# Values of the first four heads later, the matmuls of two heads kept together for scores and for values, and the second norm's weights turned with the last forget sums

## The chip, the cores and the metric

The kernel runs on one core of one Trainium2 chip. The metric is the device time of one execution in microseconds (us), as the median of several runs of the same kernel. A core has five engines with instruction streams of their own, which wait for each other by semaphores: TensorE (PE in the profile; PEld is its weight load), VectorE (DVE), ScalarE (ACT), GpSimd (POOL) and SyncE (SP). DMA transfers are issued from the streams of SP, ACT and POOL.

## The reference

One inference step of a trunk with two layers, for 256 rows of a new stream (the prompt) and 8 running streams of 16 rows each (the sample), 384 rows in all and 2048 columns. Layer 0 projects the normed rows into eight forgetting-attention heads (fox) and eight stick-breaking heads, with queries, keys, values and gates, and writes keys and values out as well. Layer 1 is a gated MLP. The change touches layer 0, and in it mostly the fox heads:

```python
def fox_core(q, k, v, Fq, Fk, qpos, kpos):
    s = jnp.einsum('bqhd,bkhd->bhqk', q, k).astype(jnp.float32) * ATTN_SCALE
    s = s + (jnp.swapaxes(Fq, 1, 2)[..., :, None] - jnp.swapaxes(Fk, 1, 2)[..., None, :])
    causal = kpos[None, :] <= qpos[:, None]
    s = jnp.where(causal, s, -jnp.inf)
    p = jax.nn.softmax(s, axis=-1)
    return jnp.einsum('bhqk,bkhd->bqhd', p.astype(v.dtype), v)
...
for layer in range(DEPTH):
    if layer % 2 == 0:
        fq, fk, fv, fz, logf_p, sq, sk, sv, sz = ab_project(rmsnorm(hp, norm0_g), w_in0, b_forget)
        fo = fox_prompt(fq, fk, fv, logf_p)
        so = sb_prompt(sq, sk, sv)
        mix = jnp.concatenate([fo * jax.nn.silu(fz), so * jax.nn.silu(sz)], axis=-1)
        hp = hp + jnp.einsum('bsn,nd->bsd', mix, w_out0)
...
        k_all = jnp.concatenate([cache_fox_k.astype(gk.dtype), gk], axis=1)
        v_all = jnp.concatenate([cache_fox_v.astype(gv.dtype), gv], axis=1)
        F_all = jnp.cumsum(jnp.concatenate([cache_fox_logf.astype(jnp.float32), logf_s], axis=1), axis=1)
        go = fox_core(gq, k_all, v_all, F_all[:, P:], F_all, qpos, kpos)
...
    else:
        u, v, z = c_project(rmsnorm(hp, norm1_g), w_in1, sgu_ln_g, sgu_ln_b)
```

F is the running sum of the log forget gates. The sample rows attend to 128 cached rows of their stream and to their own; `norm1_g` is the weight vector of the second norm.

## The kernel before

**Projections.** Weights come from DRAM in pieces of 128 rows by 512 columns (`raw`, five buffers, SP's queue, L74). ACT rounds each to a high part (`whi`, L84) and DVE takes the rest as a low part (`wlo`, L86); the activations are split in the same way. `dense_nat` goes over the rows k of a weight two at a time, and `products` makes three products for each of the three blocks of 128 rows (prompt, prompt, sample): high by high (L100), high by low (L101), low by high (L102), 18 products for each pair of pieces, each 128x512. The text counts these large products to say where in PE's stream something stands.

**Quads.** `quad(g)` handles four heads: g = 0 and 1 are fox heads, 2 and 3 stick-breaking ones. It projects k, (v for g = 0), q, z, (v for g > 0). The work on the heads is put between the products of later projections: `at(g, what, kp, f)` registers f to be called in `dense_nat` of that quad and projection ahead of the pair of pieces kp (`between`). The table `places` says where each quad's four pieces go: scores of heads 0 and 1, scores of heads 2 and 3, then `attended` for the two pairs.

**A head** is a generator (`head`), driven by `scores` and `attended`. Its first part reads the running sums spread over the partitions (`fb`, L608 to L611, POOL's queue) and turns cached keys. Its second issues the prompt's score matmuls (L626, L627, L629), its third the cached ones (L632), the softmax (DVE L644, L645, L650, ACT L648) and the store of the attention weights to DRAM (`wd`, L667, ACT's queue). `scores` then reads them back in blocks for both heads of a pair (L492, four transfers on POOL's queue). The fourth part turns these blocks with DVE (L670, tile `PT`). The fifth makes the sample's value matmuls (L678 with own values, L682 with cached ones), the last the prompt's (L684 to L686) and the gating (L689). After it the result is stored (L504), and the cached values of a later head are read (L464). `mix_split` later splits a quad's gated results into high and low parts for the output projection.

**Forget sums.** For quad 0, `forget` is a generator that is called between products of the v projection. Its middle part sums the log forget gates by matmuls with a triangular matrix (L358 to L363 and two groups of four at L373), its last part transposes the sums (L383). Small matmuls write to PSUM banks from a pool of four (`bank`). `gains(j)` transposes the weights of norm j (PE, L164) into such a bank and copies them (DVE, L165) to `gT`.

**What sets the order.** The program is written in the Tile framework, whose scheduler orders the instructions of each engine by a model of their time and inserts the waits. `tc.issue_after(i)` is a context: what is written in it is put behind instruction i in the order of its own engine, which adds no wait of its own between engines.

Of the kernel before, what the change touches and what calls it, by code (L numbers as in the profile page):

```python
# [18 lines left out]
NT = 3  # L19
# [18 lines left out]
def tile_hybrid_step(  # L38
# [8 lines left out]
    V, S, G, PE = nc.vector, nc.scalar, nc.gpsimd, nc.tensor  # L47
# [45 lines left out]
    def products(out, his, los, ws, kp, tbs, first, last):  # L93

        for tb in tbs:
            t = slice(tb * P, (tb + 1) * P)
            for j, (hi, lo) in enumerate(ws):
                k = kp + j
                o = out[tb]
                PE.matmul(o, lhsT=his[k][:, t], rhs=hi[:, 0, :], start=(k == first), stop=False)  # L100
                PE.matmul(o, lhsT=his[k][:, t], rhs=lo[:, 0, :], start=False, stop=False)  # L101
                mm = PE.matmul(o, lhsT=los[k][:, t], rhs=hi[:, 0, :], start=False, stop=(k == last))  # L102
        return mm

    def dense_nat(w, k0, c0, his, los, nk=None, between=None, out=None, ks=None):


        nk = nk or len(his)
        out = out or [dbank() for _ in range(NT)]
        for kp in range(0, nk, 2) if ks is None else ks:  # L110
            behind = ()
            if between and kp in between:
                with tc.issue_after(splits[-1]), tc.issue_after(highs[-1]):
                    behind = between[kp]() or ()
            ws = [wunit(w[(k0 + k) * P:(k0 + k + 1) * P, c0:c0 + 512], 1, 512, behind=behind) for k in (kp, kp + 1)]
            products(out, his, los, ws, kp, range(NT), 0, nk - 1)
        return out

    def turn(src, dst, trn=None):
# [37 lines left out]
    with ExitStack() as l0:  # L157
# [4 lines left out]
        def gains(j):  # L162
            gb = bank()
            PE.transpose(gb[:, :KT], graw[:, j, :], ident[:KT, :KT])  # L164
            return V.tensor_copy(gT[:, j * KT:(j + 1) * KT], gb[:, :KT])  # L165
# [177 lines left out]
        def forget(o):  # L343
            z = lc.tile([P, NT, 8], F32, name="fz")
            for tb in range(NT):
                V.scalar_tensor_tensor(out=z[:, tb, :], in0=o[tb][:, 256:264], scalar=rstd[:, tb:tb + 1], in1=bfg, op0=ALU.mult, op1=ALU.add)
            e = lc.tile([P, NT, 8], F32, name="fe")
            S.activation(e, z, AF.Abs)
            S.activation(e, e, AF.Exp, scale=-1.0)
            S.activation(e, e, AF.Ln, bias=1.0)  # L350
            V.scalar_tensor_tensor(out=logf, in0=z, scalar=0.0, in1=e, op0=ALU.min, op1=ALU.subtract)
            G.dma_start(flf_p.rearrange("o (t p) h -> p (o t) h", p=P), logf[:, :2, :])
            G.dma_start(flf_s.rearrange("b q h -> (b q) h"), logf[:, 2, :])

            yield
            gains(1)
            b3 = bank()
            PE.matmul(b3[:8, :2 * P], lhsT=logf[:, 0, :], rhs=UT, start=True, stop=False)  # L358
            PE.matmul(b3[:8, P:2 * P], lhsT=logf[:, 1, :], rhs=UT[:, :P], start=False, stop=True)
            bs = bank()  # L360
            PE.matmul(bs[:8, :P], lhsT=logf[:, 2, :], rhs=BT, start=True, stop=True)
            for b_ in range(8):
                PE.matmul(bs[:8, P + b_:P + b_ + 1], lhsT=clf[:, b_, :], rhs=ones[:, 0:1], start=True, stop=True)  # L363
            tot = lc.tile([8, 8], F32, name="ftot")
            V.tensor_copy(tot, bs[:8, P:P + 8])
            FT = lp.tile([8, 2 * T], F32, tag="pr", name="FT")[:, :T]
            V.tensor_copy(FT[:, :2 * P], b3[:8, :2 * P])
            V.tensor_tensor(out=FT[:, 2 * P:].rearrange("h (b q) -> h b q", q=16), in0=bs[:8, :P].rearrange("h (b q) -> h b q", q=16),
                            in1=tot.unsqueeze(2).broadcast_to([8, 8, 16]), op=ALU.add)
            for hg in range(2):  # L370
                b5 = bank()
                for hh in range(4):
                    PE.matmul(b5[:8, hh * P:(hh + 1) * P], lhsT=clf[:, :, 4 * hg + hh], rhs=UT[:, :P], start=True, stop=True)  # L373
                hs = slice(4 * hg, 4 * hg + 4)
                b5v = b5[:8].rearrange("b (h p) -> b h p", p=P)
                nFc = lp.tile([8, 4, P], F32, tag="KT", bufs=4, name=nm("nFc"))
                S.activation(nFc, b5v, AF.Copy, scale=-1.0)
                G.dma_start(nFcd[:, hs, :], nFc)
            yield
            b4 = bank()  # L380
            for tb in range(NT):
                PE.transpose(b4[:, tb * 8:(tb + 1) * 8], FT[:, tb * P:(tb + 1) * P], ident[:8, :8])
            V.tensor_copy(Fnat, b4[:, :24].rearrange("p (t h) -> p t h", h=8))  # L383
            nFT = lp.tile([8, 2 * T], F32, tag="PT", name="nFT")[:, :T]
            V.tensor_scalar(out=nFT, in0=FT, scalar1=-1.0, scalar2=None, op0=ALU.mult)
            G.dma_start(nFd, nFT)
# [49 lines left out]
        def at(g, what, kp, f):  # L436
            plan.setdefault((g, what), {}).setdefault(kp, []).append(f)
# [28 lines left out]
        def quad(g):  # L466
# [11 lines left out]
            def scores(pair):  # L478

                for hh in pair:  # L480
                    hs = slice(hh * P, hh * P + P)
                    own[hh] = head(g, h0 + hh, own["k"][:, hh], lambda hs=hs: own["v"][:, :, hs], own["q"][:, hh],
                                   keys_of[4 * g + hh], lambda n=4 * g + hh: values_of[n], lambda hs=hs: own["z"][:, :, hs])
                wd = own[pair] = dram.tile([2, 6, P, P], F32, name=nm("wd"))
                for hh in pair[::-1]:
                    next(own[hh])
                for _ in range(2):
                    for j, hh in enumerate(pair):
                        own[hh].send(wd[j])
                blk = own["blk", pair] = slot(F32).rearrange("p (j x) -> p j x", j=2)  # L490
                for j in range(4):
                    G.dma_start(blk[32 * j:32 * j + 32].rearrange("p j (a d) -> p (j a) d", d=32),  # L492
                                wd[:, :, :, 32 * j:32 * j + 32].rearrange("j x (a p) d -> p (j x a) d", p=32))
                for hh in pair:
                    cached_keys(4 * g + hh + 2)

            def attended(pair):
                for j, hh in ((1, pair[1]), (0, pair[0])):
                    own[hh].send(own["blk", pair][:, j, :])
                for hh in pair:  # L500
                    next(own[hh])
                for hh in pair:
                    next(own[hh], None)
                    G.dma_start(own["d"][hh].rearrange("(t p) c -> p t c", p=P), own["z"][:, :, hh * P:hh * P + P])  # L504
                for hh in pair:
                    cached_values(4 * g + hh + 2)
                if pair[0]:
                    mixed.append(blocks(own["d"])[0])


            places = ((("z", 12), ("k", 2), ("k", 8), ("k", 12)), (("z", 12), ("v", 2), ("k", 2), ("k", 8)))[g > 0]
            at(g, "q", 2 if g == 0 else 14, lambda: turned("k"))
            at(g, "z", 12, lambda: turned("q"))
            for i, (what, kp) in enumerate(places):
                at(g + (what == "k"), what, kp, lambda i=i: (scores, attended)[i // 2](((0, 1), (2, 3))[i % 2]))
            at(g + 1, "q", (12, 8, 8, 8)[g], lambda: mix_split())

            def evict(o, dst, scale, n=512):
                for tb in range(NT):
# [67 lines left out]
        def mix_split():  # L587
            blk = mixed.pop(0)
            mT = big("vnat").rearrange("p t c -> p (t c)").rearrange("p (k t) -> p k t", k=4)
            V.transpose(out=mT.rearrange("p k t -> p (k t)"), in_=blk.rearrange("p k t -> p (k t)"))  # L590
            hi, lo = slot().rearrange("p (k t) -> p k t", k=4), slot().rearrange("p (k t) -> p k t", k=4)
            for k in range(4):
                S.activation(hi[:, k, :], mT[:, k, :], AF.Copy)
                V.tensor_tensor(out=lo[:, k, :], in0=mT[:, k, :], in1=f32(hi[:, k, :]), op=ALU.subtract)
                mh.append(hi[:, k, :])
                ml.append(lo[:, k, :])
# [4 lines left out]
        def head(g, h, kT, values, qT, kc, vc, gate):  # L601
# [65 lines left out]
            nc.scalar.dma_start(wd.rearrange("x q k -> q x k"), weights.rearrange("q (x k) -> q x k", k=P))  # L667
            blk = yield
            PT = lp.tile([P, 2 * T], F32, tag="PT", name=nm("PT"))
            V.transpose(out=PT, in_=blk)  # L670
            yield
            PD = PT[:, T:]
            vn, vc, z = values(), vc(), gate()
            ob = bank()
# [317 lines left out]
```

## Time and profile before

| | us |
|---|---|
| runs | 1812.33, 1813.67, 1812.5 |
| median of the three | 1812.5 |
| profiled execution, its own time | 1815.39 |
| its span, from the first to the last instruction | 1813.7 |
| mean granted TensorE clock over the span | 0.995 |

The profiled execution is one more run of the same kernel, with the profiler on; its time contains 1.7 us beside the span. In its rows "a<-b" is an output tile and its inputs, "x8" the number of instructions taken together, and a bracket at the end of a timeline row holds the idle time of the engine just before, and whose end it waited for. The profile's line numbers are those of the kernel before; in the changed kernel the same lines stand 2 or 3 further down, except in the forget sums, where the shift is 1 (L373 is L374) after `gains(1)` is gone.

### The profile page before, as it was taken

How to read it: one execution, taken by the hardware profiler on the slowest of the kernel's cores; microseconds unless marked ns; L12 is line 12 of the kernel's file. 1: busy time of each engine (PE TensorE's matmuls, PEld its weight loads, DVE VectorE, ACT ScalarE, POOL GpSimd, SP SyncE). 2: the span in 40 equal slices, each digit the busy share in tenths (PEclk: the TensorE clock that was granted, in tenths of full speed). 3: DMA queues.
4: the chain of work that ended last, by engine and by line, in shares of the span. 5: the costliest groups of instructions: out<-in, count | busy, mean ns of one | idle time of the engine just before them, and what ended most of it. 6: DMA issues, size and time to landing. Idle time of an engine off the chain costs nothing. (4 is left out here: it accounts for less than half of the span.)

```text
span 1813.7 us, 24384 instructions
## 1 busy us (share of the span) xinstructions
PE 1788.8 (99%) x8575; PEld 1483.8 (82%) x8575; DVE 924.2 (51%) x1538; ACT 710.2 (39%) x1261; POOL 369.9 (20%) x544
## 2 busy tenths in 40 slices
PE   9999799999999999999999999999999999999998
PEld 8988588888888888888888888888888888888887
DVE  6337356458448455543433544554544563455366
ACT  5435236337337344433333333333333333333334
POOL 1515524313312202200300120320130210220020
PEclk9999899999999999999999999999999999999999
DMA  6868778878876877644444444454544554555553
GB/s 195 233 179 212 201 216 216 251 196 206 238 207 179 241 204 207 189 128 128 135 129 131 138 137 146 148 146 130 157 143 128 146 154 128 145 146 150 164 145 117
DMA packets 185771, 307.63 MB, mean 170 GB/s; under 512 B 22904, under 2 KB 63152, under 8 KB 185648
## 3 DMA queue, kind: packets, MB, share of 16 engines
q1 hardware_dynamic: 127696, 225.37, 42.1%
q0 software_dynamic: 25072, 63.53, 14.1%
q10 hardware_dynamic: 32880, 17.18, 3.2%
q8 instruction: 67, 1.10, 0.3%
q14 instruction: 56, 0.46, 0.1%
HBM read 269.23 MB, written 30.47 MB: 165 GB/s over the span
## 5 line engine op out<-in xcount | busy, mean ns | idle before, releaser
L86 DVE TENSOR_TENSOR wlo<-raw,whi 128x512 fp32r<-128x512 f32 x784 | 538.0, 695 | 745.1 <-ACT whi L84 744.9
L101 PE MATMUL d<-wlo,slot 128*128 128x512 f32 x2349 | 916.6, 391 | 0.2
L102 PE MATMUL d<-whi,slot 128*128 128x512 f32 x2349 | 912.0, 389 | 0.0
L84 ACT ACTIVATE whi<-raw 128x512 fp32r<-128x512 f32 x784 | 493.4, 631 | 944.9 <-PE d L102 889.3
L100 PE MATMUL d<-whi,slot 128*128 128x512 f32 x2349 | 822.9, 391 | 0.0
L100 PEld LDWEIGHTS d<-whi,slot 128*128 128x128 f32 x2349 | 440.9, 188 | 94.3 <-ACT whi L84 1.6
L101 PEld LDWEIGHTS d<-wlo,slot 128*128 128x128 f32 x2349 | 441.0, 188 | 91.7 <-DVE wlo L86 1.0
L102 PEld LDWEIGHTS d<-whi,slot 128*128 128x128 f32 x2349 | 441.0, 188 | 91.5
L126 POOL DMA_DIRECT2D gTt<-trn x128 | 78.0, 618 | 446.0 <-issue 263.9
L396 POOL DMA_DIRECT2D slot<-d x48 | 44.1, 924 | 145.9 <-DVE wlo L86 53.6
L492 POOL DMA_DIRECT2D slot<-wd x32 | 29.4, 924 | 103.4 <-DMA wd<-pr 34.6
L833 POOL DMA_DIRECT2D wr<-in_w_sp_dram x64 | 34.9, 553 | 26.2 <-DVE wT L837 25.1
L826 DVE TENSOR_TENSOR slot<-d,slot 128x512 f32<-128x512 f32 x48 | 32.0, 686 | 12.4 <-PE d L102 12.4
L783 POOL DMA_DIRECT2D slot<-in_sgu_ln_g_dram x8 | 4.5, 567 | 135.5 <-PE d L102 135.5
L455 POOL DMA_DIRECT2D kcache<-in_cache_sb_k_dram x32 | 24.9, 786 | 32.4 <-DVE KT L621 32.4
L455 POOL DMA_DIRECT2D kcache<-in_cache_fox_k_dram x32 | 25.0, 789 | 23.4 <-DVE KT L621 22.2
L709 POOL DMA_DIRECT2D blk<-h1d x12 | 11.0, 919 | 70.7 <-DMA h1d<-slot 60.4
L799 POOL DMA_DIRECT2D bcol<-in_b_sp_dram x1 | 1.2, 1176 | 116.1 <-DVE w L798 116.1
L862 PE MATMUL a<-vt,wT 128*128 128x256 f32 x96 | 24.5, 380 | 0.0
L777 POOL TENSOR_SCALAR rsv<-mvr 128x3 f32<-128x3 f32 x1 | 0.5, 540 | 113.0 <-DVE mvr L776 113.0
L774 DVE BATCH_NORM_STATS2 stats<-vt 128x6 f32<-128x512 f32 x24 | 16.3, 690 | 11.4 <-ACT vt L773 11.4
L849 DVE SCALAR_TENSOR_TENSOR gate<-d,rstd,gate 128x512 f32<-128x512 f32 x24 | 17.4, 748 | 7.3 <-PE d L102 7.3
(239 smaller groups left out, 1201.3 us busy)
## 6 DMA issues: line engine op xcount, KB each, us to landing
raw<-in_w_in_dram SPq DMA_DIRECT2D x640, 256.0 KB, 2.8
raw<-in_w_out_dram SPq DMA_DIRECT2D x189, 256.0 KB, 3.4
slot<-d POOLq DMA_DIRECT2D x48, 192.0 KB, 6.2
d<-slot ACTq DMA_DIRECT2D x24, 256.0 KB, 3.9
wd<-pr ACTq DMA_DIRECT2D x16, 384.0 KB, 5.8
slot<-wd POOLq DMA_DIRECT2D x32, 192.0 KB, 5.3
gTt<-trn POOLq DMA_DIRECT2D x128, 48.0 KB, 3.5
kcache<-in_cache_fox_k_dram POOLq DMA_DIRECT2D x32, 128.0 KB, 5.8
```

Source lines behind the costliest of these rows:

```text
L84: highs.append(S.activation(hi, raw, AF.Copy).ins)
L86: splits.append(V.tensor_tensor(out=lo, in0=raw, in1=f32(hi), op=ALU.subtract).ins)
L100: PE.matmul(o, lhsT=his[k][:, t], rhs=hi[:, 0, :], start=(k == first), stop=False)
L101: PE.matmul(o, lhsT=his[k][:, t], rhs=lo[:, 0, :], start=False, stop=False)
L102: mm = PE.matmul(o, lhsT=los[k][:, t], rhs=hi[:, 0, :], start=False, stop=(k == last))
L126: G.dma_start(dst[32 * j:32 * j + 32, :, 32 * a:32 * a + 32], trn[32 * a:32 * a + 32, :, 32 * j:32 * j + 32])
L396: r = G.dma_start(blk[32 * j:32 * j + 32].rearrange("p h (a d) -> p (h a) d", d=32), d[:, :, 32 * j:32 * j + 32].rearrange("h (a p) d -> p ...
L455: G.dma_start(k[32 * j:32 * j + 32].rearrange("p (b d) -> p b d", d=32), (c_fox_k, c_sb_k)[n // 8][:, :, n % 8, 32 * j:32 * j + 32].rearra ...
L492: G.dma_start(blk[32 * j:32 * j + 32].rearrange("p j (a d) -> p (j a) d", d=32), wd[:, :, :, 32 * j:32 * j + 32].rearrange("j x (a p) d -> ...
L826: evicted = V.tensor_tensor(out=h1[c][:, tb, :], in0=o[tb], in1=h1[c][:, tb, :], op=ALU.add)
L833: G.dma_start(wr[js, 0, :].rearrange("p (a s) -> p a s", s=32), w_sp[g, :, js].rearrange("(a p) s -> p a s", p=32))
L862: PE.matmul(m[:, i * 256:(i + 1) * 256], lhsT=wTs[i][:, tb // 2, :], rhs=vt[:, tb, cs], start=True, stop=True)
```

## The change

Four things are changed. `gains(1)` moves from the head of the forget sums to behind the last forget transposes. In `scores`, the prompt's score matmuls of both heads of a pair are put behind the last large product that had been written. In `attended`, the matmuls of the first head are put behind the turning of both heads' weights. And the places of quad 0 change: `attended` of heads 0 and 1 from k, 8 of the next quad to k, 12, that of heads 2 and 3 from k, 12 to q, 4, and the first quad's `mix_split` from q, 12 to z, 4. The places of the other quads stay (they are written in another form).

```diff
+    last_product = []
...
-            products(out, his, los, ws, kp, range(NT), 0, nk - 1)
+            last_product[:] = [products(out, his, los, ws, kp, range(NT), 0, nk - 1).ins]
...
             yield
-            gains(1)
             b3 = bank()
...
             V.tensor_copy(Fnat, b4[:, :24].rearrange("p (t h) -> p t h", h=8))
+            gains(1)
...
                 for hh in pair[::-1]:
                     next(own[hh])
-                for _ in range(2):
-                    for j, hh in enumerate(pair):
-                        own[hh].send(wd[j])
+                with tc.issue_after(last_product[0]):
+                    for hh in pair:
+                        next(own[hh])
+                for j, hh in enumerate(pair):
+                    own[hh].send(wd[j])
...
             def attended(pair):
-                for j, hh in ((1, pair[1]), (0, pair[0])):
-                    own[hh].send(own["blk", pair][:, j, :])
-                for hh in pair:
-                    next(own[hh])
+                turned = [own[hh].send(own["blk", pair][:, j, :]) for j, hh in ((1, pair[1]), (0, pair[0]))]
+                with tc.issue_after(turned[0].ins), tc.issue_after(turned[1].ins):
+                    for hh in pair:
+                        next(own[hh])
...
-            places = ((("z", 12), ("k", 2), ("k", 8), ("k", 12)), (("z", 12), ("v", 2), ("k", 2), ("k", 8)))[g > 0]
+            places = (((0, "z", 12), (1, "k", 2), (1, "k", 12), (1, "q", 4)), ((0, "z", 12), (0, "v", 2), (1, "k", 2), (1, "k", 8)))[g > 0]
...
-            for i, (what, kp) in enumerate(places):
-                at(g + (what == "k"), what, kp, lambda i=i: (scores, attended)[i // 2](((0, 1), (2, 3))[i % 2]))
-            at(g + 1, "q", (12, 8, 8, 8)[g], lambda: mix_split())
+            for i, (later, what, kp) in enumerate(places):
+                at(g + later, what, kp, lambda i=i: (scores, attended)[i // 2](((0, 1), (2, 3))[i % 2]))
+            at(g + 1, *(("z", 4) if g == 0 else ("q", 8)), lambda: mix_split())
...
             PT = lp.tile([P, 2 * T], F32, tag="PT", name=nm("PT"))
-            V.transpose(out=PT, in_=blk)
-            yield
+            yield V.transpose(out=PT, in_=blk)
```

In PE's stream at the forget sums there stood, before (`a` is a bank, `graw` the norm weights as loaded, `sums` the triangular matrix, `logf` and `clf` the log forget gates of the rows and of the cache):

```order
L164 MATMUL a_936<-ident,graw 128x16
L358 MATMUL a_939<-sums,logf 8x256
L359 MATMUL a_939<-sums,logf 8x128
L361 MATMUL a_942<-sums,logf 8x128
L363 MATMUL a_942<-ones,clf 8x1 x8
L373 MATMUL a_957<-sums,clf 8x128 x4
L373 MATMUL a_965<-sums,clf 8x128 x4
```

At the later place, among the products of the v projection (`d` is the bank of a product, 256 columns wide here) and behind the transposes of the sums (`FT`), PE's stream of the changed kernel has:

```order
L427 MATMUL d_839<-wlo_1021,slot_135 128x256
L428 MATMUL d_839<-whi_1020,slot_136 128x256
L383 MATMUL a_1042<-ident,FT 128x8 x3
L166 MATMUL a_1047<-ident,graw 128x16
L426 MATMUL d_837<-whi_1055,slot_135 128x256
```

The norm's transpose (L164, now L166) has left the head of the sums, whose other rows keep their order, and stands as the last small matmul behind the transposes of L383.

The value matmuls of heads 2 and 3 stood in PE's stream, before, behind the 867th large product (the tiles of the number 361 and 362 are the two heads' cached values, `PT` the turned weights):

```order
L100 MATMUL d_397_2157<-whi_410_2198,slot_12_129 128x512
L101 MATMUL d_397_2157<-wlo_411_2200,slot_12_129 128x512
L102 MATMUL d_397_2157<-whi_410_2198,slot_13_130 128x512
L678 MATMUL a_377_2033<-vnat_104_611,PT_376_2031 32x128 x4
L682 MATMUL a_377_2033<-vcache_361_1965,PT_376_2031 32x128 x8
L678 MATMUL a_378_2046<-vnat_104_611,PT_375_2029 32x128 x4
L682 MATMUL a_378_2046<-vcache_362_1967,PT_375_2029 32x128 x8
```

In PE's stream of the changed kernel the same matmuls stand here, behind the 943rd:

```order
L101 MATMUL d_392_2106<-wlo_426_2284,slot_16_133 128x512
L102 MATMUL d_392_2106<-whi_425_2282,slot_17_134 128x512
L100 MATMUL d_392_2106<-whi_428_2288,slot_16_133 128x512
L681 MATMUL a_407_2171<-vnat_104_611,PT_406_2169 32x128 x4
L685 MATMUL a_407_2171<-vcache_373_2025,PT_406_2169 32x128 x8
L681 MATMUL a_408_2184<-vnat_104_611,PT_405_2167 32x128 x4
L685 MATMUL a_408_2184<-vcache_374_2027,PT_405_2167 32x128 x8
```

They follow 76 large products later, in the next quad's q projection instead of its k projection. The value matmuls of heads 0 and 1 stood behind the 813th and the 825th product and now stand together behind the 819th.

On DVE, before, the turning of the first pair's blocks (L670) stood among the low parts of the weights, well ahead of the second pair's softmax (`z`, L644):

```order
L86 TENSOR_TENSOR wlo_356_1901<-raw_354_1897,whi_355_1899 128x512
L670 STREAM_TRANSPOSE PT_357_1921<-slot_285_1604 128x768
L670 STREAM_TRANSPOSE PT_358_1923<-slot_285_1604 128x768
L86 TENSOR_TENSOR wlo_365_1973<-raw_363_1969,whi_364_1971 128x512
L86 TENSOR_TENSOR wlo_368_1979<-raw_366_1975,whi_367_1977 128x512
L86 TENSOR_TENSOR wlo_371_2003<-raw_369_1999,whi_370_2001 128x512
L86 TENSOR_TENSOR wlo_374_2009<-raw_372_2005,whi_373_2007 128x512
L644 SCALAR_TENSOR_TENSOR z_327_1779<-a_322_1764,Fnat_565,fb_318_1751 128x256
```

On DVE of the changed kernel it stands directly ahead of it:

```order
L86 TENSOR_TENSOR wlo_365_1955<-raw_363_1951,whi_364_1953 128x512
L86 TENSOR_TENSOR wlo_368_1961<-raw_366_1957,whi_367_1959 128x512
L674 STREAM_TRANSPOSE PT_369_1981<-slot_285_1604 128x768
L674 STREAM_TRANSPOSE PT_370_1983<-slot_285_1604 128x768
L648 SCALAR_TENSOR_TENSOR z_327_1779<-a_322_1764,Fnat_565,fb_318_1751 128x256
```

Four splits of weights now come ahead of the two turns that came behind them. The second pair's own turns move as well, from behind the low part `wlo_411` to behind that of `wlo_429`, which the last product shown above its value matmuls belongs to. On POOL the two reads of cached values (L464) of the first pair now stand together, ahead of the second `fb` reads (L608).

Score matmuls: the prompt's three of the first head of the second pair stood behind the 711th, 712th and 715th product and stand behind the 729th with those of the other head; the other quads' second pairs move by 18 products in the same way.

## The prediction

> **What bounds the kernel now.** I read the page first, then PE's waits, then the places that they name. Rows give busy time and the mean of one in ns.
>
> ```profile
> span 1813.7 us, 24384 instructions
> PE 1788.8 (99%) x8575; PEld 1483.8 (82%) x8575; DVE 924.2 (51%) x1538; ACT 710.2 (39%) x1261; POOL 369.9 (20%) x544
> L101 PE MATMUL d<-wlo,slot 128*128 128x512 f32 x2349 | 916.6, 391 | 0.2
> ```
>
> TensorE is busy 99% of the span, every other engine half of it or less. The line L101 is one of three equal ones (L100, L101, L102): 7047 products in all, and L101 had waited 0.2 us in the whole run. So the kernel is one long stream of products; only what interrupts the stream or is added to it counts. The waits of PE are few (total in us, times, longest):
>
> ```profile
> PE a L678 <- DVE PT L670: 13.5, 1, 13.5
> PE a L373 <- DVE gT L165: 1.3, 1, 1.3
> PE a L196 <- DVE ones L132: 1.1, 1, 1.1
> PE a L219 <- DMA slot<-in_x_sample_dram: 0.3, 1, 0.3
> ```
>
> That is the whole list, 16.2 us. The first two lie on what is changed: the value matmuls of the second pair of heads (heads 2 and 3 of the first four), and the forget sums behind norm1's weights. The last two stand at the start and are left alone. The timeline around the first (start, duration, instruction, idle time before it and who ended it):
>
> ```profile
> 194.95 0.39 PE L102 MATMUL d<-whi,slot 128*128 128x512 f32 x1
> 195.63 0.39 PE L102 MATMUL d<-whi,slot 128*128 128x512 f32 x1
> ...
> 200.46 3.70 POOL L492 DMA_DIRECT2D slot<-wd  x4 [9.53 <-DMA wd<-pr]
> 207.64 1.84 DVE L670 STREAM_TRANSPOSE PT<-slot 128x768 f32<-128x768 f32 x2 [12.41 <-DMA slot<-wd]
> 209.53 0.65 PE L678 MATMUL a<-vnat,PT 128*32 128x128 f32 x8 [13.51 <-DVE PT L670]
> 214.32 0.48 PE L100 MATMUL d<-whi,slot 128*128 128x512 f32 x1
> ```
>
> Three products start within 195.63 - 194.95 = 0.68 us, so a product takes 0.227 us of the stream (its printed 0.39 overlaps the next). In a stream that does not stop, such value matmuls start 0.32 us after the last product (320.90 to 321.22, below); here that would be 195.63 + 0.32 = 195.95. The attention weights of the pair were being stored to DRAM (wd), are read back in blocks by four POOL transfers (L492, from 200.46), turned by DVE (207.64 to 209.48), and only then do the value matmuls start, at 209.53; products go on at 214.32.
>
> **Term 1: the second pair's values go 76 products later.** Before, these matmuls stand behind the 867th product, in the changed order behind the 943rd. 76 x 0.227 = 17.2 us of work now comes ahead of them, so the need moves from 195.95 to 213.2. Their data was ready at 209.53. The stop was 13.58 us long, and it goes if the data comes no more than 3.6 us later against the stream. It also left a cold array behind:
>
> ```profile
> 195.90:200.10 4.20, 0.12 (x1) 0.00 (x0) 0.00 (x0) 0.34 (x1) 0.00 (x0) 1.00 0.90 268
> 200.10:207.20 7.10, 0.00 (x0) 0.00 (x0) 0.00 (x0) 0.00 (x0) 6.41 (x8) 0.50 0.60 159
> 207.20:214.40 7.20, 4.87 (x61) 4.32 (x61) 2.30 (x4) 0.00 (x0) 1.81 (x2) 0.54 0.24 59
> 320.90 0.39 PE L102 MATMUL d<-whi,slot 128*128 128x512 f32 x1
> 321.22 0.43 PE L678 MATMUL a<-vnat,PT 128*32 128x128 f32 x8
> 324.03 0.47 PE L100 MATMUL d<-whi,slot 128*128 128x512 f32 x1
> 324.34 0.39 PE L101 MATMUL d<-wlo,slot 128*128 128x512 f32 x1
> ```
>
> In the three windows (length; busy time of PE, its weight loads, DVE, ACT, POOL; granted clock, DMA share, GB/s) the clock is still 1.00 for 4.2 us after the last product, then 0.50, and 0.54 while the matmuls of the pair run: 209.53 to 214.32 is 4.79 us. The same group for two heads in the next quad, in a warm stream, takes 321.22 to 324.03 = 2.81. The difference, **1.98 us**, goes with the stop. Together 13.58 + 1.98 = **15.56 us**.
>
> The Trainium skill, "TensorE: Matmul & The Clock Gate", section "What's actually happening", says that an idle window of about 3.4 us lets the clock fall to half. The windows agree on the half clock and put its onset 4.2 us after the stop; by that section's figure a new wait would turn cold somewhat sooner than I reckon below, which leaves the sum as it is.
>
> **Term 2: norm1's weights move behind the forget sums.** Before, their transpose (L164) and its DVE copy (L165) stand ahead of the sums, and the second group of L373 waits for that copy.
>
> ```profile
> 73.32 1.03 PE L373 MATMUL a<-sums,clf 128*8 128x128 f32 x8
> 75.69 1.05 PE L373 MATMUL a<-sums,clf 128*8 128x128 f32 x8 [1.33 <-DVE gT L165]
> 76.66 0.39 PE L424 MATMUL d<-whi,slot 128*128 128x256 f32 x1
> ```
>
> The eight matmuls of the second group take 76.66 - 75.69 = 0.97 us; the first group, started at 73.32, would have been through at 74.29. Lost: **1.40 us**. In the new order no matmul of the sums has L165 ahead of it; the transpose is one instruction wherever it stands, and at its new place the next matmuls are projection products with banks of their own, so its copy is covered by them. If the wait came back there, it would cost the same 1.4.
>
> **Term 3: matmuls kept together.** Small matmuls between products cost a changeover each time. For values the first pair stood in two places:
>
> ```profile
> 180.01 0.39 PE L101 MATMUL d<-wlo,slot 128*128 128x512 f32 x1
> 182.12 0.39 PE L101 MATMUL d<-wlo,slot 128*128 128x512 f32 x1
> 184.42 0.39 PE L102 MATMUL d<-whi,slot 128*128 128x512 f32 x1
> 186.54 0.39 PE L101 MATMUL d<-wlo,slot 128*128 128x512 f32 x1
> ```
>
> Each stretch holds two products and one head: 2.11 - 0.45 and 2.12 - 0.45, together 3.33 us. The two heads in one place, 320.90 to 324.34, hold two products as well: 3.44 - 0.45 = 2.99. Gain **0.34 us**, once; the other pairs stood together already. For scores, the changed order puts the two heads' prompt matmuls in one place for four second pairs. What that is worth the trace does not show, as no pair stands together; here is part of one such stretch:
>
> ```profile
> 154.32 0.59 PE L100 MATMUL d<-whi,slot 128*128 128x512 f32 x1
> 154.74 0.38 PE L627 MATMUL a<-kT,qT 128*128 128x128 f32 x2
> 155.66 0.38 PE L629 MATMUL a<-kT,qT 128*128 128x128 f32 x2
> 156.12 0.39 PE L102 MATMUL d<-whi,slot 128*128 128x512 f32 x1
> ```
>
> From 154.32 to 156.12 are five products (1.13) and four small matmuls, which so cost 0.67; at 0.12 each (0.97 / 8 in L373) they would cost 0.48. The gain is then at most 0.19 in each of four places, 0.8 in all; that they come somewhat later and all at once could cost as much at the other end, since softmax starts some 18 products later there. I take **0.2**, 0.05 a place, nearer to nothing than to the 0.17 a head that the values show, since each score matmul is longer than the small value ones and hides more of a changeover; I keep -0.8 to 0.8 for the range.
>
> **What is late next.** Sum: 15.56 + 1.40 + 0.34 + 0.2 = **17.5 us**, if the data of the second pair is there at its new place. What runs ahead is now 1.74 us shorter (terms 2 and 3), so the need is at 213.2 - 1.74 = 211.5. The chain before it: softmax, store of wd (L667), L492, DVE. Two things push it. DVE now turns the first pair's weights (1.84 us for two) directly ahead of the second pair's first softmax instruction, while the stream comes 1.40 earlier: some 0.4 us later. And the four L492, which ran while no weights were being fetched, now share the DMA with a stream that goes on. From issue to landing (least, median, most):
>
> ```profile
> DMA to landing us min/median/max: 3.5/5.3/8.2
> DMA to landing us min/median/max: 3.6/3.9/4.0
> DMA to landing us min/median/max: 6.7/10.4/14.2
> DMA to landing us min/median/max: 5.5/8.0/9.4
> ```
>
> These are: all 32 L492; the four in the stop; the two wd stores of this pair; the weight loads (L74) from 184 to 196. With the median 5.3 in place of 3.9 the data comes 1.4 later, with 0.4 from DVE at 209.53 + 1.8 = 211.3, which is 0.2 before the need. So I cost the wait at nothing, and say that it is close: with the 8.2 of the slowest, 214.2 and a wait of 2.7. If the store itself lands later by as much as its two landings differ from their mean (3.8), the data is late by 3.6 at the median. Behind the waiting matmuls stand the products in PE's order, and behind L670 the splits of the next weights in DVE's, so a wait there stops everything. The other moved pieces (the mixing of the first quad 72 products later, the loads of cached values that now stand together on POOL, the stores L504 of both heads) have no row in the list of waits before, and I cost them at nothing; their cover is the product stream, and a miss shows as a new row there.
>
> **The rivals.**
> - *A: a smaller wait stays at the new place.* The numbers just given: 0.5 to 4.2 us. Over 4.2 the clock falls, and the group costs 1.98 more. Time 1795.5 to 1801. For it: 0.2 us to spare, a DMA share of 0.90 already at 195.90 to 200.10. Against it: one load fewer in the way, as the cached values are asked for earlier, ahead of the crowd.
> - *B: the products wait for weights.* Loads landed in 5.5 to 9.4 us in the crowd, and one arrived just in time:
>
> ```profile
> 193.88 0.63 ACT L84 ACTIVATE whi<-raw 128x512 fp32r<-128x512 f32 x1 [0.58 <-DMA raw<-in_w_in_dram]
> 194.54 0.69 DVE L86 TENSOR_TENSOR wlo<-raw,whi 128x512 fp32r<-128x512 f32 x1 [0.52 <-ACT whi L84]
> ```
>
>  A load serves nine products (2.04 us); five buffers, each held about 1.4 us after landing by the two splits, give one load per (landing + 1.4) / 5. At 9.4 that is 2.16, 0.12 too slow; at 12 it is 2.68, and ten such loads lose 6.4 us. Before, the stop let the DMA empty itself; now it does not. Time 1796 to 1801.5.
> - *C: slower than before.* The same mechanism in its extreme, at the same place: to eat 17.5 us and 3.6 more, ten loads in a row would need 4.15 us each, a landing of 19.4 us. The highest row for any transfer there is 14.2, for another queue. Time above 1816.
> - *D: no change: PE's stream isn't the limit,* and the products only run at the pace at which weights come; what is saved at two stops comes back as waits elsewhere. 1812.5. Against it: 0.2 us of waiting at L101 in the whole run, and products at an even 0.227. The Trainium skill, "TensorE: Matmul & The Clock Gate", section "Back-to-back issue gap", gives about 131 ns for each of a stream of 512-column matmuls; by that figure our 227 ns would be paced by something else, which is this rival. The trace disagrees: no wait is on record behind these 227 ns.
>
> **How the numbers follow.** The profiled run took 1815.4 us (span 1813.7 and 1.7 around it); 1815.4 - 17.5 = 1797.9. That run lies 2.9 above the median of the three timed ones, 1812.5, and these lie within 1.3 of each other. Against the median: 1812.5 - 17.5 = **1795**. Chances: the forecast 0.60 (own range 1793.5 to 1796.5), A 0.27, B 0.05, C 0.04, D 0.04. The range takes A and B in: 1792.5 (0.6 more from scores, the spread of the runs, a shorter changeover) to 1801. About 0.2% (3.6 us) is what a measurement tells from no change: faster 0.92 (forecast, A, B), same 0.04 (D), slower 0.04 (C).
>
> **What would show it.** In the profile after: the row of PE waiting for the turned weights (L670 before) gone or under 1 us, else A; the row of L373 waiting for L165 gone; a mean clock of 1.00 throughout 195 to 215; first-pair values in one place; no row of PE or of a split waiting for raw weights, else B. If the rows are gone and the time isn't, D. The forecast fails first at the landing of L492 and of the store ahead of it.

## The result and the profile after

| | before, us | after, us |
|---|---|---|
| median of five runs each | 1813.67 | 1797.66 |
| lowest and highest | 1812.33, 1813.8 | 1796.31, 1799.46 |
| profiled execution, its own time | 1815.39 | 1799.46 |
| its span | 1813.7 | 1797.8 |
| mean granted TensorE clock | 0.995 | 0.998 |

The ratio of the times is 0.9916, with a 95% interval of 0.9902 to 0.9929: 16.0 us less. The forecast was 17.5 us less and 1795; the measured 1797.66 is inside the range.

The page of the kernel after, first its head and the line of the products (busy time, mean ns | idle time before them, who ended it):

```profile
span 1797.8 us, 24388 instructions
PE 1787.1 (99%) x8575; PEld 1482.9 (82%) x8575; DVE 923.8 (51%) x1538; ACT 710.4 (40%) x1261; POOL 370.2 (21%) x544
L101 PE MATMUL d<-wlo,slot 128*128 128x512 f32 x2349 | 916.2, 391 | 1.2 <-DVE wlo L86 1.0
```

Then the whole list of PE's waits after:

```profile
PE a L198 <- DVE ones L134: 1.1, 1, 1.1
PE d L101 <- DVE wlo L86: 1.0, 1, 1.0
```

The rows of the turned weights (13.5 us) and of the norm's weights (1.3 us) are gone, as is the 0.3 us at the start, which comes and goes between executions of kernels whose start is the same. A row has come: once, a product waits 1.0 us for the low part of a weight. The line L101 shows the same microsecond as idle time, 1.2 us where 0.2 stood.

The place where the stream stopped, after (rows taken from the timelines of DVE and PE):

```profile
207.27 1.84 DVE L674 STREAM_TRANSPOSE PT<-slot 128x768 f32<-128x768 f32 x2 [0.64 <-DMA slot<-wd]
211.68 0.39 PE L100 MATMUL d<-whi,slot 128*128 128x512 f32 x1
212.00 0.43 PE L681 MATMUL a<-vnat,PT 128*32 128x128 f32 x8
214.81 0.47 PE L101 MATMUL d<-wlo,slot 128*128 128x512 f32 x1
```

The turned weights are ready at 207.27 + 1.84 = 209.11, and PE comes to them at 212.00: 2.9 us to spare. The group takes 214.81 - 212.00 = 2.81 us, the warm price, where it took 4.79. The windows of the same stretch (length; PE, its weight loads, DVE, ACT, POOL; granted clock, DMA share, GB/s):

```profile
195.90:200.10 4.20, 4.20 (x20) 3.48 (x19) 2.08 (x3) 1.56 (x3) 4.19 (x5) 1.00 1.07 312
200.10:207.20 7.10, 7.10 (x33) 5.87 (x32) 3.12 (x4) 1.90 (x3) 2.35 (x3) 1.00 1.01 227
207.20:214.90 7.70, 7.70 (x83) 6.41 (x82) 4.18 (x7) 1.90 (x3) 6.81 (x9) 1.00 0.79 197
```

PE is busy throughout at a clock of 1.00, and the DMA share, which fell in the stop before (0.60 and 0.24), is now 1.0 for eleven microseconds.

To see what each place gave, I took the start of the same large product in the traces of both kernels, both counted from their first product of this kind (L100 to L102), since that one starts between 8.6 and 10.7 us into the span in different executions. Before, the 3000th after the first starts 789.42 us after it, in the changed kernel 773.23: 16.19 less. (The 288 products of the v projection, 256 columns wide, are not in this count, so the 867th product of the text above is the 579th here.) The table has the difference between the two traces in the even stretches of products on both sides of each place:

| place in the stream | forecast, us | measured, us |
|---|---|---|
| forget sums | 1.40 | 1.60 |
| scores of second pairs, four places | 0.2 | 0.31 (0.05, 0.05, 0.10, 0.10) |
| first pair's values in one place | 0.34 | 0.02 |
| second pair's values: stop and cold group | 15.56 | 15.57 |
| mixing of the first quad | 0 | -1.29 |
| sum, with 0.01 lost at the start | 17.5 | 16.20 |

### The profile page after: what moved, and what is told of

Its sections match the earlier page's. It is cut to its first block, busy times and chain, and to the rows that moved or that the text cites. A ratio compares the mean times of both kernels' runs of the same rounds, so it can differ in the third digit from the quotient of the medians.

```text
span 1797.8 us, 24388 instructions
## 1 busy us (share of the span) xinstructions
PE 1787.1 (99%) x8575; PEld 1482.9 (82%) x8575; DVE 923.8 (51%) x1538; ACT 710.4 (40%) x1261; POOL 370.2 (21%) x544
## 5 line engine op out<-in xcount | busy, mean ns | idle before, releaser
L101 PE MATMUL d<-wlo,slot 128*128 128x512 f32 x2349 | 916.2, 391 | 1.2 <-DVE wlo L86 1.0
L102 PE MATMUL d<-whi,slot 128*128 128x512 f32 x2349 | 912.0, 389 | 0.0
L100 PE MATMUL d<-whi,slot 128*128 128x512 f32 x2349 | 821.4, 390 | 0.0
L100 PEld LDWEIGHTS d<-whi,slot 128*128 128x128 f32 x2349 | 440.9, 188 | 94.4 <-ACT slot L584 0.8
L101 PEld LDWEIGHTS d<-wlo,slot 128*128 128x128 f32 x2349 | 441.0, 188 | 93.3 <-DVE wlo L86 2.4
L102 PEld LDWEIGHTS d<-whi,slot 128*128 128x128 f32 x2349 | 440.9, 188 | 91.7
L712 POOL DMA_DIRECT2D blk<-h1d x12 | 10.9, 918 | 70.8 <-DMA h1d<-slot 60.5
```

## The experiments

Each run is timed beside runs of the kernel before. "Product time" below is the time from the first large product to the 3000th after it in the profile (before 789.42, after 773.23); it leaves out what comes ahead of the first product, and each of two kernels that were profiled twice gave the same product time within 0.1 us. The timed medians of one kernel spread more than that, so the small parts are read from it.

### One part alone: the norm's weights

```diff
             yield
-            gains(1)
             b3 = bank()
...
             V.tensor_copy(Fnat, b4[:, :24].rearrange("p (t h) -> p t h", h=8))
+            gains(1)
```

> The kernel before with only the norm weights' transpose moved behind the last forget transposes. Theory (each stop is a loss of its own): PE's row of L373 waiting for L165 disappears, and the whole comes 1.4 to 1.6 us earlier than before. Rival (the later stop is set by a chain of its own): the stop ahead of the second pair's values ends at the same time as before, so it grows by the same 1.4 us from 13.5, and the time does not change (within 0.3).

Measured: 1812.47 against 1813.84, ratio 0.9991 (0.9982 to 1.0). Product time 787.53, 1.89 less. PE's waits of this run:

```profile
PE a L678 <- DVE PT L670: 13.5, 1, 13.5
PE a L196 <- DVE ones L132: 1.1, 1, 1.1
PE d L251 <- DVE slot L226: 0.4, 1, 0.4
```

The row of the norm's weights is gone and the stop is as long as before. What was gained ahead of it was not swallowed: 0.20 us are lost among the first products, 1.60 gained at the forget sums, and the other 0.49 lie in the cold group, which took 4.31 here (206.78 to 211.09) in place of 4.79. The timed ratio alone, whose interval reaches 1.0, could not tell this. The chain that ends the stop came earlier by as much as PE did. The rival falls; the term adds up with the others.

### One part alone: the places

The lines of `places`, of the loop under it and of `mix_split` as in the change, nothing else.

> The kernel before with only the places of the first quad changed (values of both pairs and the mixing). Theory: the stop of 13.5 us and its cold array go (15.6 to 15.8 us), the 1.3 us wait of the forget sums stays, and a wait of about 1 us for the low part of a weight stands in the next quad's z projection, behind the transpose for the mixing: 14.4 us less than before. Rival (the store of the second pair's weights landed earlier in the changed kernel only because of the grouped matmuls): without the grouping the store lands about 14 us after its issue as before, the values wait 1 to 3 us at the new place, and the gain is 11.5 to 13.5 us.

Measured: 1799.65 against 1813.84, ratio 0.9921 (0.9907 to 0.9934). Product time 774.94, 14.48 less. The stop is gone without the grouping, worth 15.57 as in the changed kernel, and PE's waits hold the norm's weights still:

```profile
PE a L373 <- DVE gT L165: 1.6, 1, 1.6
PE a L196 <- DVE ones L132: 1.1, 1, 1.1
PE d L425 <- DVE wlo L91: 0.3, 1, 0.3
```

The rival with the grouping falls: the second store of wd was issued at 186.12 and landed at 196.99, 10.9 us, without it, and the values had 1.4 us to spare. The wait behind the mixing, which I expected here too, did not come: the transpose waited 2.0 us on DVE for its data, not 4.7, and PE lost nothing there. That 14.48 agrees with the 14.4 expected is therefore chance: 1.11 us were lost earlier, in the v projection, 0.8 of it around the wait of L425 for a low part and 0.3 at the longer wait of L373. The values of the first pair stand in one place here as well, so it is their place that puts them together, not the ordering edge.

### One part alone: the ordering edges

The edges in `scores` and `attended`, with the places and `gains` as before.

> The kernel before with only the two ordering edges (scores and values of a pair). Theory: scores kept together gain nothing that can be seen, 0.0 to 0.3 us, and the value matmuls of the first pair stay in two places, so the time is that of before within 0.5 us, with the stop of 13.5 us as before. Rival (together saves a changeover at each place): 0.8 us less. Second rival (later scores delay the second pair's softmax and its store): the stop of 13.5 grows by up to 4 us, the first head's scores being 18 products later.

Measured: 1813.5 against 1813.84, ratio 0.9996 (0.9987 to 1.0004). Product time 788.66, 0.76 less, of which 0.36 is the wait of the forget sums (1.0 in this profile where 1.3 stood) and 0.31 the four places of the scores (0.05, 0.05, 0.10, 0.10). The stop is 13.7 us, not longer for the later scores. So the edges on the scores are worth 0.3 us and can't be seen in the time; those on the values did nothing at the old place.

### The mixing later

```diff
-            at(g + 1, *(("z", 4) if g == 0 else ("q", 8)), lambda: mix_split())
+            at(g + 1, *(("z", 8) if g == 0 else ("q", 8)), lambda: mix_split())
```

> The changed kernel with the first quad's mixing two steps (36 products, 8.2 us) later. Theory (the transpose for the mixing waits 4.7 us for its data at the head of DVE's queue and holds two splits of weights behind it): the 1.0 us wait of L101 for a low part goes, 1.0 to 1.2 us less than the changed kernel. Rival (the wait belongs to a late weight transfer, since the DMA is crowded there): a wait of about 1 us stays at the same product, and the time does not change (within 0.3).

In the changed kernel DVE and PE at the new wait look like this:

```profile
231.89 0.69 DVE L86 TENSOR_TENSOR wlo<-raw,whi 128x512 fp32r<-128x512 f32 x1 [2.13 <-ACT whi L84]
237.26 1.78 DVE L594 STREAM_TRANSPOSE vnat<-slot 128x1536 f32<-128x1536 f32 x1 [4.68 <-DMA slot<-d]
238.97 1.25 DVE L86 TENSOR_TENSOR wlo<-raw,whi 128x512 fp32r<-128x512 f32 x2
239.67 0.50 PE L101 MATMUL d<-wlo,slot 128*128 128x512 f32 x1 [1.00 <-DVE wlo L86]
```

DVE has done its last split at 232.58, and the next in its order is the transpose for the mixing, whose data lands at 237.2. Two splits of weights stand behind it; the first is done about 239.6, and PE has run out by then. With the mixing two steps later, DVE shows:

```profile
231.94 1.37 DVE L86 TENSOR_TENSOR wlo<-raw,whi 128x512 fp32r<-128x512 f32 x2 [2.13 <-ACT whi L84]
235.11 0.69 DVE L86 TENSOR_TENSOR wlo<-raw,whi 128x512 fp32r<-128x512 f32 x1 [1.80 <-ACT whi L84]
236.70 0.69 DVE L86 TENSOR_TENSOR wlo<-raw,whi 128x512 fp32r<-128x512 f32 x1 [0.89 <-ACT whi L84]
237.31 1.77 DVE L594 STREAM_TRANSPOSE vnat<-slot 128x1536 f32<-128x1536 f32 x1
```

The transpose starts at the same time, with no wait, and the two splits that it held back (the second of the row at 231.94 and the one at 235.11) come ahead of it, with one more. PE's list has no row for a low part. Product time 771.92, 1.31 less than the changed kernel, 17.50 less than before. The time is 1796.43 against 1813.84, ratio 0.9902 (0.9889 to 0.9916). The rival of a late weight transfer falls: the wait goes though no transfer of weights was moved.

### The second pair's values back at the old place

```diff
-            places = (((0, "z", 12), (1, "k", 2), (1, "k", 12), (1, "q", 4)), ...
+            places = (((0, "z", 12), (1, "k", 2), (1, "k", 12), (1, "k", 14)), ...
```

This puts them behind the same product as before; the mixing stays at z, 8.

> The changed kernel, its mixing at z, 8 as in the run before, with the values of heads 2 and 3 put back behind the 867th product. Theory (the stop comes from the place alone, and in the changed order the store of the weights lands some 5 us earlier after its issue, so that the read back starts earlier): a stop at those matmuls of 9 to 11 us, a cold group after it if the stop passes 4.2 us, 11 to 13 us more than that run. Rival (the early landing of the store belongs to the later place, too): the store lands some 14 us after its issue as before, the stop is 13 to 15 us, and the time is that of the kernel before less 2 to 3 us.

Measured: 1812.27 against 1814.49, ratio 0.9984 (0.9975 to 0.9993). The stop is back in PE's waits, and the timeline shows its end:

```profile
PE a L681 <- DVE PT L674: 12.6, 1, 12.6
PE a L198 <- DVE ones L134: 1.1, 1, 1.1
```

```profile
203.57 1.84 DVE L674 STREAM_TRANSPOSE PT<-slot 128x768 f32<-128x768 f32 x2 [11.99 <-DMA slot<-wd]
205.46 0.65 PE L681 MATMUL a<-vnat,PT 128*32 128x128 f32 x8 [12.56 <-DVE PT L674]
```

Product time 787.23, 15.31 more than with the values late. So this one place carries the change. Of the expectations neither holds whole: the store landed 10.3 us after its issue (183.44 to 193.71) and not 14, as the theory had it, but the stop is 12.6 and not 9 to 11. I had reckoned with a read back as quick as in the stop before (3.9 us from issue to landing); its four parts took 5.5 to 5.9. The store was also issued only 9.5 us ahead of the start of the stop (192.90), where it had been 10.5 before (185.53 to 196.02).

### The cached values behind the store

The first edit called the reads of cached values two steps later, with the mixing at z, 8:

```diff
-                for hh in pair:
+                for hh in pair if g or pair[0] else ():
                     cached_values(4 * g + hh + 2)
...
+            if g == 0:
+                at(1, "k", 14, lambda: [cached_values(n) for n in (2, 3)] and None)
```

> The changed kernel, its mixing at z, 8, with the two reads of cached values behind the second pair's store of attention weights instead of ahead of it, as one of them stood before. Theory (what is asked for around the store shares the DMA with it and delays it): the second store of wd lands 12 to 15 us after its issue instead of 9.3, the turned weights are ready 3 to 5 us later, the 2.9 us of slack at the values are used up, and 0 to 2 us are lost there. Rival (the store's landing has other reasons): it lands within 1.5 us of the 9.3, no wait at the values, time unchanged.

Measured: 1796.7 against 1814.49, ratio 0.9896 (0.988 to 0.9913). It moved nothing: the reads were still issued at 181.44 and 182.47, ahead of the store at 184.92. It is no test of the theory. The second edit gives POOL's order an edge:

```diff
-                    G.dma_start(own["d"][hh].rearrange(...), own["z"][:, :, hh * P:hh * P + P])
-                for hh in pair:
-                    cached_values(4 * g + hh + 2)
+                    stored = G.dma_start(own["d"][hh].rearrange(...), own["z"][:, :, hh * P:hh * P + P])
+                with tc.issue_after(stored.ins) if g == 0 and pair[0] == 0 else ExitStack():
+                    for hh in pair:
+                        cached_values(4 * g + hh + 2)
```

> As the run before with the cached values late, but with an ordering edge on POOL that really puts the two reads behind the first pair's stores, and so behind the issue of the second pair's store of attention weights; the values of that pair stand 4 products later. Theory (transfers asked for after the store delay it): the second store of wd lands 12 to 15 us after its issue instead of 9.3 to 10.9, the turned weights come 2 to 5 us later, and up to 2 us are lost at the values. Rival (the store's landing has other reasons): 9 to 11 us, and the time of the run with the mixing at z, 8 within 1 us.

Measured: 1797.5 against 1813.26, ratio 0.9909 (0.9893 to 0.9926); product time 772.19. Now the reads are issued at 186.80 and 187.70, behind the store at 184.03. From issue to landing (least, median, most), the two stores of wd in the changed kernel, in this run, and then the four reads back in the changed kernel and in this run:

```profile
DMA to landing us min/median/max: 4.7/7.0/9.3
```

```profile
DMA to landing us min/median/max: 5.5/5.5/5.6
```

```profile
DMA to landing us min/median/max: 7.0/7.9/8.6
```

```profile
DMA to landing us min/median/max: 8.5/9.4/10.0
```

Both expectations are wrong. The store lands in 5.6 us, sooner than in any other profile, though both large reads are asked for after it; as far as one profile can show, it was the reads asked for ahead of it that held it up in the changed kernel. The read back then takes longer, with the two reads of cached values now in flight beside it, and in the end the turned weights are ready at 207.76 (205.93 + 1.83), 3.8 us ahead of PE, which comes 4 products (0.9 us) later here. The product time hardly changes (0.27 more, all of it among the first products). Why the store of the kernel before took 14.2 us, with one of the two reads ahead of it and one behind, these runs leave open.

### The changed kernel and the later mixing, once more

> The changed kernel itself once more. Theory (the transpose for the mixing is on the edge of its data's landing): L101 waits 0 to 1.5 us for a low part in the next quad's z projection, and the time is 0.5 to 1.3 us above the run with the mixing at z, 8. Rival (the wait of the first profile was a chance of that one execution): no such wait, and no difference between the two in this call.

> The changed kernel with the mixing at z, 8 once more, beside the changed kernel on the same chip. Theory: 0.5 to 1.3 us less than the changed kernel, no wait for a low part. Rival: the same time within 0.3 us.

Measured together: the changed kernel 1797.42, ratio 0.991 (0.9895 to 0.9925); with the mixing at z, 8 1797.06, ratio 0.9909 (0.9894 to 0.9923). The wait is there again in the changed kernel's profile (its row of PE's waits, then DVE's timeline) and again not in the other's:

```profile
PE d L101 <- DVE wlo L86: 1.1, 1, 1.1
```

```profile
235.31 1.78 DVE L594 STREAM_TRANSPOSE vnat<-slot 128x1536 f32<-128x1536 f32 x1 [4.74 <-DMA slot<-d]
```

Product times: 773.31 (773.23 the first time) and 771.91 (771.92). At the place of the mixing the two kernels differ by 1.29 and by 1.40 us in the two pairs of profiles. The timed medians differ by 1.23 the first time, when the two were timed apart, and by 0.36 the second, with some 2.5 us to each side of every median by the intervals of the ratios, so that the time of the whole program shows no difference between them. The later mixing is no slower than the changed kernel, and its stream is 1.3 to 1.4 us shorter; that the whole program is faster by it is not shown by the times.

## Why the prediction was right, and where it was not

**The bound and term 1 were right.** The kernel is one stream of products; the stop of 13.58 and the cold group went together (15.57 measured, 15.56 forecast), and putting the place back brought 15.31 back. That the size is met so closely is luck in part, since the cold group is not the same in each execution. In the four profiles with the stop (before, the norm's weights alone, the edges alone, the values back at the old place) it took 4.79, 4.31, 4.51 and 5.30 us. The granted clock had come back to 1.00 at 4.2, 3.2, 3.7 and 5.7 us after its start; and it had fallen to 0.50 at 4.1, 3.1, 3.7 and 4.6 us after the stop began. The 4.2 that the prediction took as the wait over which the clock falls is thus one execution's, and no threshold.

**Term 2 was right, and 0.2 too small:** 1.40 forecast, 1.60 measured both alone and in the changed kernel, 1.67 gained at the sums and 0.07 lost at the transpose's new place. The prediction counted the wait alone and let the transpose itself cost the same wherever it stands; and nothing at the new place waits for the copy.

**Term 3 was mis-sized.** "Gain **0.34 us**, once" measured 0.02. I compared with a group of the next quad, where the sample's matmuls of both heads stand together and then the prompt's. In the changed kernel the first pair stands like this:

```profile
180.21 0.39 PE L102 MATMUL d<-whi,slot 128*128 128x512 f32 x1
180.53 0.43 PE L681 MATMUL a<-vnat,PT 128*32 128x128 f32 x8
180.77 0.62 PE L685 MATMUL a<-vcache,PT 128*32 128x128 f32 x16
181.32 0.49 PE L687 MATMUL a<-vnat,PT 128*128 128x128 f32 x2
181.74 0.43 PE L681 MATMUL a<-vnat,PT 128*32 128x128 f32 x8
181.98 0.62 PE L685 MATMUL a<-vcache,PT 128*32 128x128 f32 x16
182.53 0.49 PE L688 MATMUL a<-vnat,PT 128*128 128x128 f32 x2
...
183.67 0.48 PE L100 MATMUL d<-whi,slot 128*128 128x512 f32 x1
```

One prompt matmul (L687) stands between the two heads' sample matmuls, so PE goes from 32-column weights (L681, L685) to 128-column ones and back and forth once more. The group takes 183.67 - 180.53 = 3.14, 0.33 more than the 2.81 of the second pair at 212.00, whose sample matmuls stand together. That is the whole gain that I had put down. The two groups have the same matmuls and differ in their order alone; that the change of shape is what costs is my reading of it, and no run tests it. The order was to be seen in the changed kernel ahead of time. The scores, for which I took 0.2 from a range of -0.8 to 0.8, gave 0.31.

**"What is late next" held, by two errors that cancel in part.** I put the need at 211.5 and the data at 211.3, on the clock of the trace before, whose first large product starts 0.48 us earlier in the span than that of the trace after (10.13 and 10.61). On that clock PE came there at 211.52 and the data at 208.63: the need was right, the data 2.7 us early. I had left the store of wd to land about when it did before (199.69); it landed at 194.65, which is 194.17 on that clock. I had given the read back its median of 5.3; its parts took 7.0 to 8.6, at a DMA share of 1.0. So rival A did not come, but the margin is small: in the seven profiles with the values at the new place it was 2.9, 1.4, 0.3, 2.1, 3.8, 1.5 and 3.0 us (the 0.3 where the store took 12.7 us from its issue, the 3.8 with the values 4 products later), and no profile shows a wait there.

**The step that failed** is the one on the other moved pieces, the mixing among them: "I cost them at nothing; their cover is the product stream, and a miss shows as a new row there." The new row is there, 1.0 us of waiting and 1.29 in the stream. A long row of products is no cover for an instruction that stands in the queue of the engine which feeds the products. The trace before had a sign of this on DVE, where the same transpose waited for the same read, at no cost to PE:

```profile
230.25 1.78 DVE L590 STREAM_TRANSPOSE vnat<-slot 128x1536 f32<-128x1536 f32 x1 [0.63 <-DMA slot<-d]
```

The mixing was not put too near to the values: DVE came to the transpose 15.3 us after the end of their group before (214.32 to 229.62) and 17.8 after (214.81 to 232.58). What grew is the way of the data, from 15.8 us (to 230.13) to 22.4 (to 237.18). The results of the heads are stored first (L504, in the changed kernel L508), and the read for the mixing is asked for only when they have landed. From issue to landing (least, median, most), the two stores before and after, then the four parts of the read before and after:

```profile
DMA to landing us min/median/max: 3.4/3.5/3.7
DMA to landing us min/median/max: 8.4/8.8/9.1
DMA to landing us min/median/max: 5.2/6.8/7.4
DMA to landing us min/median/max: 4.7/6.6/8.3
```

So some 5 us of the 6.6 come from the stores. In the 5.7 us behind the values the DMA share was 0.55 before and 1.01 after. The stores took 2.7 to 4.1 us in all four profiles with the stop, where the DMA share was 0.02 to 0.29 while the values ran at a clock of 0.50, and 5.1 to 9.1 in all seven without it. So the stop that the change removes had also made these transfers quick. With the mixing 36 products later, PE does not wait for it in any of four profiles, though DVE still waits 0.5 and 1.2 us in two of them (those of the two edits on the cached values), and the stream is 17.50 us shorter than before. That this is the forecast sum is luck, for two errors inside it cancel: 0.32 too much for the first pair's values against 0.20 and 0.11 too little for the forget sums and the scores.

**The rest of the distance** from 1795 to 1797.66 is, beside the 1.29 of the mixing, the spread of the runs: the five of after lie between 1796.31 and 1799.46, and the five of before have a median 1.2 us above that of the three that I subtracted from.

**The rivals B, C and D** did not come: no row of PE for high parts or raw weights (ACT waited for raw weights once between 190 and 245, 0.9 us, and PE did not feel it), and at D's place, the products kept their 0.227 us (211.45 to 211.68 in the trace after) while the time fell.

## What to carry to other kernels

When a change removes a stop, reckon the transfers behind it anew: here they had landed quickly only while the stop left the DMA free. And look at each engine's own order for what stands behind an instruction that waits for a transfer: an engine that is half idle still stops the busy one if such an instruction is ahead of what feeds it. Ahead of a sum from one stop, ask whether the chain that ends it moves with the stream; here it did. And the price of a group of small matmuls, taken from another place, held here only where the order inside the group was the same (2.81 against 3.14 us).

## What was unexpected of the hardware

The order in which transfers were asked for went with large differences in landing. The store of 384 KB landed in 5.6 us in the one profile with two large reads asked for 2.8 and 3.7 us after it, and in 9.3 to 12.7 us in the seven other profiles in which the first pair's values stand at their new place, with the same reads ahead of it (9.3, 10.9, 12.7, 10.3, 10.6, 10.6 and 9.4). This does not say that a later transfer never delays an earlier one: in the three profiles with those values at their old places one read was asked for 4.0 us ahead of the store and one 0.5 to 1.2 us after it, and the store took 14.0 to 14.2 us. The first large product started between 8.6 and 10.7 us into the span in executions of kernels whose start is the same, which is as much as most of the single parts of this change are worth.
